# Ten gate tiles of an input projection computed as five pairs of tiles by Strassen's identity

## The chip, the cores and the metric

One core of one Trainium2 chip runs the whole kernel. The metric is device time in microseconds of one execution. All tensors are fp32. A product of two fp32 matrices is done on TensorE as three fp32r products: each operand is first split into a high part (`hi`, a rounded copy that ScalarE writes) and a low part (`lo = x - hi`, which VectorE writes), and then hi·hi, hi·lo and lo·hi are added in PSUM. The profile calls the engines PE (TensorE), PEld (its weight loads), DVE (VectorE), ACT (ScalarE), POOL (GpSimd) and SP (SyncE, which only issues DMAs here).

## The reference, cut to what matters

One decoder layer over L = 1088 columns: 1024 prompt positions and 8 x 8 sample tokens (16 meta tokens stand ahead of them).

```
u = rmsnorm(h, norm_mix)
z = u @ w_in + b_in                       # 48 tiles of 128 columns
a, c, q, k, v, g = split(z)               # g: 24 tiles, three gates of 1024
y_a = pool_mixer(a)                       # moving means, windows 2, 4, 8, 16
y_b = silu(layernorm(conv31(glu(c)))) @ w_conv_out
y_c = attention(q, k, v) @ w_attn_out
gates = sigmoid(g).reshape(.., 3, 1024)
h = h + (gates[0]*y_a + gates[1]*y_b + gates[2]*y_c) @ w_out
h = h + square(relu(rmsnorm(h) @ w_up)) @ w_down
```

A gate tile is thus a product of a 1024x128 block of `w_in` with `u` (1024 x 1088), plus a bias. The kernel stores it in DRAM (`gD`) and reads it back when the gate is used.

## The kernel before

The program order is written by hand: an engine executes its instructions in the order in which the code issues them, and no scheduler changes it. Waits between engines are semaphores; a buffer that is used again waits for its last reader.

**Projection.** `u` lies in SBUF as eight split tiles `Uh[k]`, `Ul[k]` (uh0..uh7, ul0..ul7), 128 rows of the 1024 each. Five tiles are done in a head that also makes `u`; the loop at L1121 does tiles 5 to 47, in the order of the list `TILES`. The last ten, tiles 38 to 47, are gate tiles (kind `z`, z6 to z15). A tile is three chunks of columns (400, 320 and 368 for a gate tile); a chunk is 8 x 3 matmuls with a 128x128 weight block, 72 for the tile. ACT adds the bias and writes `zs` (L916), and the chunk is stored. The weight tile (128x1024) is loaded two tiles ahead, split once (ACT hi at L90, DVE lo at L91), two pairs of buffers.

**What runs beside it.** After each chunk `slot(natt, ndve)` issues one step from the queue `attq` (attention, later the LayerNorm of the convolution) and two from `dveq` (the 31 taps of the depthwise convolution of each of four channel groups, L444 and L446 on DVE, one pair for a tap, and the moving sums of the pooling branch, L463 to L472). The last steps of `attq` are those of the sample attention; then `tail_slices` loads the attention output `oD` and splits it (`Ox`, tiles oh and ol). When the last convolution is through, `after_conv` puts the LayerNorm steps into `attq`.

**After it.** The stage after the projection multiplies the attention output by `w_ao` and the pooled tiles by `w_pool`, multiplies by gates, and adds (AO stage). Then come the conv output, `w_out`, and the MLP.

**Strassen in the MLP.** The up projection already runs in pairs of tiles with seven products in place of eight: `load_pair` loads the two weight tiles of a pair, `sum_pair` makes four sums of 128x512 halves on POOL (L1271 to L1277), `prep` splits one of seven 128x512 operands three products ahead (ACT and DVE, both by the helper `split`, L153 and L154), `product` issues 24 matmuls of 128x272. The operands on the side of the tokens, halves of 544 columns, are split once for all pairs. Evictions (L1590 to L1604) go to ACT and DVE by turns.

Of the kernel before, what the change touches and what calls it, by code (L numbers as in the profile page):

```python
# [7 lines left out]
F32 = mybir.dt.float32  # L8
# [4 lines left out]
P = 128  # L13
# [25 lines left out]
SMP = [0] * 8 + [1] * 6  # L39

# [71 lines left out]
def hybrid_trunk_kernel(ctx, tc, I, O):  # L112
# [56 lines left out]
    W = Weights(nc, pool, page, jobs)  # L169
# [261 lines left out]

    def conv_steps(j):
# [17 lines left out]
    def pool_steps(g):  # L450
# [5 lines left out]
        def add(n, h):  # L456
            def go():
                if n < 2:
                    box[n] = (page("pt"), apool.tile([P, 8, 23], F32, name="pts", tag="pts", bufs=2))
# [16 lines left out]
        dveq.extend([add(n, 1 << n) for n in range(g + 1)] + [fin])  # L476
# [191 lines left out]
    def sample_slices():  # L668
# [3 lines left out]
        def build():  # L672
# [20 lines left out]
            box["os"] = page("os")[:, :512].rearrange("p (j t) -> p j t", j=8)  # L693

        def load(sq):
            r = page("skv")
            kr, vr = r[:, :256].rearrange("p (a s) -> p a s", a=2), r[:, 256:512]
# [18 lines left out]
        def qk(sq):  # L716
# [7 lines left out]
            lg = page("slg")[:, :192]  # L724
# [119 lines left out]
    def proj_open(ti):  # L844
# [5 lines left out]
        elif kind == "c":  # L850
            t["e"] = page("ext")
            t["s"] = apool.tile([P, 8, 38], F32, name="exts", tag="exts", bufs=2)
# [4 lines left out]
        elif kind == "a":  # L857
            t["e"] = page("ea")
            t["s"] = apool.tile([P, 8, 23], F32, name="eas", tag="eas", bufs=2)
# [59 lines left out]
    def proj_close(ti):  # L919
# [31 lines left out]
        elif kind == "q":  # L951
# [65 lines left out]
    def load_split(dst, key, src):  # L1017
        box = {}

        def ld():  # L1020
            box["t"] = page("ld")
# [9 lines left out]
    def tail_slices():  # L1031
        both = lambda *fs: (lambda: [f() for f in fs])
        idle = lambda: None
        pairs = [load_split(Ox, "o", oD[j]) for j in range(8)]
        out = [both(pairs[j][0], pairs[j + 1][0]) for j in (0, 2)]
        for j in range(0, 8, 2):
            fs = [pairs[j][1], pairs[j + 1][1]]
            fs += [pairs[j + 4][0], pairs[j + 5][0]] if j + 4 < 8 else []
            out.append((both(*fs), 1))
        return out  # L1040
# [80 lines left out]
    for ti in range(NHEAD, 48):  # L1121
        if ti == LAST_A + 1:
            dveq.append(after_conv)
        proj_open(ti)
        W.split_to(ti + 2)
        if ti == 47:
            load_gate(2, 0)
            load_gate(0, 0)
        for ci in range(3):
            proj_chunk(ti, ci)  # L1130
            slot(1, NDVE[0] if attq else NDVE[1])
        proj_close(ti)
    while len(Ox) < 8:
        slot(1, 1)
# [79 lines left out]
    apool_ctx.__exit__(None, None, None)  # L1214
    pool2 = ctx.enter_context(tc.tile_pool(name="sb2", bufs=1, reuse_waits="tile"))

    def page2(name):
        return pool2.tile([P, T], F32, name=name, tag="page2", bufs=5)

    HL = L // 2  # L1220
    hD = dram.tile([8, P, L], F32, name="hD")
    BX = ("B11", "T1", "T2", "B22", "T3", "B21", "T4")
# [40 lines left out]

    def sum_pair(j, n):
        a, b = raws[j]
        if n == 0:
            Ssum[j] = page2("s12"), page2("s34")
        s12, s34 = Ssum[j]
        S1, S2, S3, S4 = s12[:, :512], s12[:, 512:1024], s34[:, :512], s34[:, 512:1024]
        if n == 0:  # L1270
            G.tensor_tensor(S1, b[:, :512], b[:, 512:], ALU.add)  # L1271
        elif n == 1:
            G.tensor_tensor(S2, S1, a[:, :512], ALU.subtract)
        elif n == 2:
            G.tensor_tensor(S4, a[:, 512:], S2, ALU.subtract)
        else:
            G.tensor_tensor(S3, a[:, :512], b[:, :512], ALU.subtract)  # L1277

    def prep(s):
        j, i = divmod(s, 7)  # L1280
        a, b = raws[j]
        s12, s34 = Ssum[j]
        src = {"A11": a[:, :512], "A12": a[:, 512:], "A22": b[:, 512:], "S1": s12[:, :512],
               "S2": s12[:, 512:1024], "S3": s34[:, :512], "S4": s34[:, 512:1024]}[ORD[i]]
        tag = ("whi", "wlo")[s % 2]
        t = pool.tile([P, 1024], F32R, name=tag, tag=tag, bufs=2)
        split(t[:, :512], t[:, 512:], src)
        WX[s] = t
        if i == 6:
            raws.pop(j)  # L1290
            Ssum.pop(j)
# [156 lines left out]
    def product(b, s, i, first):  # L1448
        t = WX.pop(s)
        for ch in range(2):  # L1450
            for k in range(4):
# [487 lines left out]
```

## Time and profile before

| | us |
|---|---|
| timed runs: median of three (lowest, highest) | 1669.98 (1669.88, 1670.55) |
| the profiled execution, its own time | 1668.48 |
| its span, first to last instruction | 1666.7 |
| PE busy | 1639.7 (98%) |
| DVE busy | 1109.2 (67%) |
| ACT busy | 748.8 (45%) |
| POOL busy | 413.0 (25%) |

Busy time is summed over the whole span. The shares of DVE, ACT and POOL are means over stages that differ: in one window of the projection DVE is busy all the time, in another a third of it. The profile's chain of waits that ended last is 90% PE.

### The profile page before, as it was taken

How to read it: one execution, taken by the hardware profiler on the slowest of the kernel's cores; microseconds unless marked ns; L12 is line 12 of the kernel's file. 1: busy time of each engine (PE TensorE's matmuls, PEld its weight loads, DVE VectorE, ACT ScalarE, POOL GpSimd, SP SyncE). 2: the span in 40 equal slices, each digit the busy share in tenths (PEclk: the TensorE clock that was granted, in tenths of full speed). 3: DMA queues.
4: the chain of work that ended last, by engine and by line, in shares of the span. 5: the costliest groups of instructions: out<-in, count | busy, mean ns of one | idle time of the engine just before them, and what ended most of it. 6: DMA issues, size and time to landing. Idle time of an engine off the chain costs nothing.

```text
span 1666.7 us, 29169 instructions
## 1 busy us (share of the span) xinstructions
PE 1639.7 (98%) x11552; PEld 1612.8 (97%) x11552; DVE 1109.2 (67%) x1811; ACT 748.8 (45%) x1424; POOL 413.0 (25%) x324
## 2 busy tenths in 40 slices
PE   8999999999999999999999999999999999999997
PEld 7999999999999999999999999999999999999997
DVE  7786767867666575453464698888887844466574
ACT  6537667467665342374243443333333533333331
POOL 1010000001010002122343655555555100023340
PEclk9999999999999999999999999999999999999998
DMA  6051221221225262353243347777776855555642
GB/s 206 16 120 39 83 67 47 68 70 51 70 79 170 93 208 96 107 214 126 80 164 132 131 162 246 246 246 245 243 243 233 323 190 182 183 187 190 232 149 82
DMA packets 132351, 250.80 MB, mean 150 GB/s; under 512 B 33428, under 2 KB 64629, under 8 KB 132213
## 3 DMA queue, kind: packets, MB, share of 16 engines
q1 hardware_dynamic: 132212, 248.92, 45.3%
q8 instruction: 91, 1.49, 0.4%
q14 instruction: 48, 0.39, 0.1%
HBM read 168.52 MB, written 80.36 MB: 149 GB/s over the span
## 4 chain that ended last, share of the span: by engine, by line
PE 90%; DVE 4%; ACT 2%; issue 1%; DMA 1%; POOL 1%; SPq 0%; DVEq 0%; ACTq 0%; POOLq 0%
PE pm L148 12%; PE pm L150 12%; PE pm L149 12%; PE m L1651 6%; PE m L1647 6%; PE m L1649 6%; PE m L1455 6%; PE m L1457 6%; PE m L1458 6%; PE pn L148 3%; PE pn L150 3%; PE pn L149 3%; PE px L622 2%; PE px L610 2%; PE qk L569 2%
## 5 line engine op out<-in xcount | busy, mean ns | idle before, releaser
L148 PE MATMUL pm<-uh,whi 128*128 128x320 f32 (+3 forms) x1008 | 337.7, 335 | 6.6 <-ACT uh L324 6.6
L149 PE MATMUL pm<-ul,whi 128*128 128x320 f32 (+3 forms) x1008 | 331.8, 329 | 0.7 <-DVE ul L325 0.7
L150 PE MATMUL pm<-uh,wlo 128*128 128x320 f32 (+3 forms) x1008 | 331.5, 329 | 0.0
L1647 PE MATMUL m<-oph,whi 128*128 128x272 f32 (+2 forms) x896 | 259.2, 289 | 2.2 <-ACT whi L90 2.2
L1651 PE MATMUL m<-oph,wlo 128*128 128x272 f32 (+2 forms) x896 | 258.8, 289 | 1.8 <-DVE wlo L91 1.8
L1649 PE MATMUL m<-opl,whi 128*128 128x272 f32 (+2 forms) x896 | 258.5, 289 | 0.0
L91 DVE TENSOR_TENSOR wlo<-wraw,whi 128x1024 fp32r<-128x1024 f32 (+1 forms) x127 | 171.1, 1347 | 103.6 <-ACT whi L90 103.5
L90 ACT ACTIVATE whi<-wraw 128x1024 fp32r<-128x1024 f32 (+1 forms) x127 | 130.1, 1025 | 202.3 <-PE m L1649 146.9
L148 PEld LDWEIGHTS pm<-uh,whi 128*128 128x128 f32 x1008 | 190.1, 189 | 8.0 <-ACT uh L324 6.6
L149 PEld LDWEIGHTS pm<-ul,whi 128*128 128x128 f32 x1008 | 190.1, 189 | 3.4 <-DVE ul L325 2.8
L150 PEld LDWEIGHTS pm<-uh,wlo 128*128 128x128 f32 x1008 | 189.9, 188 | 0.2
L1647 PEld LDWEIGHTS m<-oph,whi 128*128 128x128 f32 x896 | 169.3, 189 | 2.6 <-ACT whi L90 2.6
L1651 PEld LDWEIGHTS m<-oph,wlo 128*128 128x128 f32 x896 | 169.2, 189 | 2.6 <-DVE wlo L91 2.5
L1649 PEld LDWEIGHTS m<-opl,whi 128*128 128x128 f32 x896 | 169.4, 189 | 0.0
L444 DVE SCALAR_TENSOR_TENSOR y<-ext,vec,y 128x1024 f32<-128x1024 f32 x120 | 154.5, 1288 | 0.0
L1455 PE MATMUL m<-bch,whi 128*128 128x272 f32 x448 | 129.0, 288 | 3.0 <-DVE cb L1598 2.5
L558 POOL TENSOR_TENSOR uq<-q,uq 128x128 fp32r<-128x128 f32 x64 | 34.7, 564 | 391.9 <-ACT uq L557 391.9
L1455 PE MATMUL m<-bch,wlo 128*128 128x272 f32 x448 | 128.8, 288 | 0.7 <-DVE cb L1598 0.7
L1458 PE MATMUL m<-bch,whi 128*128 128x272 f32 x448 | 128.9, 288 | 0.0
L1458 PE MATMUL m<-bch,wlo 128*128 128x272 f32 x448 | 128.9, 288 | 0.0
L1457 PE MATMUL m<-bcl,wlo 128*128 128x272 f32 x448 | 128.8, 288 | 0.0
L1457 PE MATMUL m<-bcl,whi 128*128 128x272 f32 x448 | 128.8, 287 | 0.0
(365 smaller groups left out, 3804.1 us busy)
## 6 DMA issues: line engine op xcount, KB each, us to landing
wraw<-w_in SPq DMA_DIRECT2D x46, 512.0 KB, 3.8
opT<-d SPq DMA_DIRECT2D x64, 272.0 KB, 3.3
ld<-opT SPq DMA_DIRECT2D x32, 544.0 KB, 4.6
wd<-w_down SPq DMA_DIRECT2D x32, 512.0 KB, 6.4
sumD<-wd SPq DMA_DIRECT2D x32, 512.0 KB, 4.9
wraw<-sumD SPq DMA_DIRECT2D x32, 512.0 KB, 3.6
gt<-gD SPq DMA_DIRECT2D x24, 544.0 KB, 4.6
ld<-opB SPq DMA_DIRECT2D x23, 544.0 KB, 4.8
```

Of the source, the lines that this page charges most:

```text
L90: self.nc.scalar.activation(hi, r, AF.Copy)
L91: self.late.append(lambda lo=lo, r=r, hi=hi: self.nc.vector.tensor_tensor(lo, r, hi.bitcast(F32), ALU.subtract))
L148: PE.matmul(ps, lhsT=wh[k], rhs=xh, start=first and i == 0, stop=False)
L149: PE.matmul(ps, lhsT=wh[k], rhs=xl, start=False, stop=False)
L150: PE.matmul(ps, lhsT=wl[k], rhs=xh, start=False, stop=last and i == n - 1)
L444: V.scalar_tensor_tensor(y[:, :NP], e[:, k:k + NP], w, y[:, :NP], ALU.mult, ALU.add)
L1455: PE.matmul(ps, lhsT=wh, rhs=xh, start=first and k == 0, stop=False, skip_group_check=True)
L1457: PE.matmul(ps, lhsT=wh, rhs=xl, start=False, stop=False, skip_group_check=True)
L1458: PE.matmul(ps, lhsT=wl, rhs=xh, start=False, stop=k == 3, skip_group_check=True)
L1647: PE.matmul(ps, lhsT=wh[:, w], rhs=xh[:, r], start=k == 0, stop=False, skip_group_check=True)
L1649: PE.matmul(ps, lhsT=wh[:, w], rhs=xl[:, r], start=False, stop=False, skip_group_check=True)
L1651: PE.matmul(ps, lhsT=wl[:, w], rhs=xh[:, r], start=False, stop=k == 15, skip_group_check=True)
```

## The change

Tiles 5 to 37 stay as they are. Tiles 38 to 47 become five pairs (numbered -5 to -1) of seven products: 35 products of 24 matmuls of 128x272, 168 matmuls for a pair. Two gate tiles share their token operand, so the identity is on the two tiles, the halves of the 1024 rows (k and k + 4), and the halves of the 1088 columns.

- `z_sums` adds hi and lo of `Uh/Ul[k]` and `[k+4]` back to fp32 (two adds of 128x1088) and makes four differences (128x544) in place. It is called for k = 0 on POOL and k = 1 on DVE when tile 36 opens, for k = 2 on POOL when tile 37 opens, and for k = 3 on DVE after tile 37.
- `z_split` splits these differences (16 splits of 128x544: ACT hi, DVE lo): T1 over the second half of `Uh/Ul[0..3]`, T2 and T3 into `za`, T4 into `zb`.
- Each product evicts two 128x272 pieces: three products on ACT, three on DVE (L1303), the last on ACT with the bias. Two stores a pair, 128x1088 each.
- Weight sums of the first pair are made on DVE, of the others on POOL. Each product has one `prep`, three products ahead.
- Behind each product stands `slot(1, 2)`: one step of `attq` (the splits of T2, T3, T4) and two of `dveq`. When the loop starts, 26 taps of the last convolution are left in `dveq`; the moving sums of the last pooling group are put ahead of them.
- The loads of `oD` and the splits `Ox` move from tiles 38 to 42 into the last pair; the last load (the eighth) is issued behind the store of the last product. `after_conv`, and with it the LayerNorm, moves behind the projection. Tile 37 runs its chunks in the order 1, 2, 0. Some small buffers become parts of pages.

The core of the diff (allocation of small buffers, and functions moved without change, left out):

```
+NZP = 5
+NZ = 48 - 2 * NZP
...
-        dveq.extend([add(n, 1 << n) for n in range(g + 1)] + [fin])
+        fs = [add(n, 1 << n) for n in range(g + 1)] + [fin]
+        if g == 3:
+            dveq[:0] = fs
+        else:
+            dveq.extend(fs)
...
-                attq.append(lambda: wide.append(0))
-                attq.extend(tail_slices())
...
+    def z_sums(k, G):
+        ua, ub = zt[k] = page("zu"), page("zu")
+        lo, hi = slice(0, HL), slice(HL, L)
+        for t, n in ((ua, k), (ub, k + 4)):
+            G.tensor_tensor(t[:, :L], Uh[n][:, NM:].bitcast(F32), Ul[n][:, NM:].bitcast(F32),
+                            ALU.add)
+        G.tensor_tensor(ua[:, lo], ua[:, hi], ua[:, lo], ALU.subtract)
+        G.tensor_tensor(ua[:, hi], ub[:, hi], ua[:, hi], ALU.subtract)
+        G.tensor_tensor(ub[:, hi], ub[:, hi], ua[:, lo], ALU.subtract)
+        G.tensor_tensor(ub[:, lo], ub[:, lo], ub[:, hi], ALU.subtract)
+
+    def z_split(x, k):
...
-    for ti in range(NHEAD, 48):
-        if ti == LAST_A + 1:
-            dveq.append(after_conv)
+    for ti in range(NHEAD, NZ):
         proj_open(ti)
         W.split_to(ti + 2)
-        if ti == 47:
+        if ti == NZ - 2:
+            z_sums(0, G)
+            z_sums(1, V)
+        if ti == NZ - 1:
+            z_sums(2, G)
+        if ti == NZ - 1:
+            load_pair(-NZP)
+        for n, ci in enumerate((0, 1, 2) if ti < NZ - 1 else (1, 2, 0)):
+            if ti == NZ - 1 and n:
+                sum_pair(-NZP, n - 1, V)
+            proj_chunk(ti, ci)
+            if ti == NZ - 1 and n:
+                prep(-7 * NZP + n - 1)
+            slot(1, NDVE[0] if attq else NDVE[1])
+        proj_close(ti)
+    while attq:
+        slot(1, 1)
+    slot(0)
+    z_sums(3, V)
...
+    load_pair(1 - NZP)
+    for k in range(4):
+        z_split("T1", k)
+    prep(-7 * NZP + 2)
+    for n in (2, 3):
+        sum_pair(-NZP, n, V)
+    for x in ("T2", "T3", "T4"):
+        attq.extend(lambda x=x, k=k: [z_split(x, k), z_split(x, k + 1)] for k in (0, 2))
+    oq = [load_split(Ox, "o", oD[j], page2) for j in range(8)]
+    for s in range(-7 * NZP, 0):
+        j, i = divmod(s, 7)
...
+        if s + 3 < 0:
+            prep(s + 3)
+        if j < -1:
+            if 2 <= i < 6:
+                sum_pair(j + 1, i - 2)
+        elif i == 0:
             load_gate(2, 0)
             load_gate(0, 0)
...
+        product(b, s, i, i in (0, 1, 5), z_comb)
...
+            if i < 3:
+                A.activation(d, ps, AF.Copy)
+            elif i == 6:
+                A.activation(d, ps, AF.Identity, bias=bias_col[1])
+            else:
+                V.scalar_tensor_tensor(d, ps, bias_col[i == 4], d, ALU.add, ALU.add)
+        if i > 4:
+            store(gD[TILES[ti + i - 5][1]], c[:, :L])
+        if i == 4 and j < -2:
+            load_pair(j + 2)
+        if j == -1:
...
+            if i > 1:
+                oq[i - 2][1]()
+            for n in (0, 1) if i == 1 else (i,) if i else ():
+                oq[n][0]()
+        slot(1, 2)
+    oq[7][0]()
+    for j in range(5, 8):
+        oq[j][1]()
+    dveq.append(after_conv)
```

Three places of the order follow. A row is line, operation, out<-in with buffer numbers, and the shape; line numbers are each kernel's own. In both kernels y is the convolution's sum (its last group here), `whi`/`wlo` are split weights, `s12` the weight sums S1 and S2.

**DVE, the turn from tile 37 to what follows it.** Before, from the lo of the weights of tile 38 on:

```order
L91 TENSOR_TENSOR wlo_6572<-wraw_6436,whi_6571 128x1024
L444 SCALAR_TENSOR_TENSOR y_4602<-ext_4600,vec_71,y_4602 128x1024
L446 SCALAR_TENSOR_TENSOR y_4602<-exts_4601,vec_71,y_4602 128x64
L444 SCALAR_TENSOR_TENSOR y_4602<-ext_4600,vec_71,y_4602 128x1024
L446 SCALAR_TENSOR_TENSOR y_4602<-exts_4601,vec_71,y_4602 128x64
```

With the change, from the weight sum S2 (ready for the second product) to the first split of T1:

```order
L1076 TENSOR_TENSOR s12_6624<-s12_6624,wraw_6574 128x512
L157 TENSOR_TENSOR whi_6701<-s12_6624,whi_6701 128x512
L453 SCALAR_TENSOR_TENSOR y_4596<-ext_4594,vec_71,y_4596 128x1024
L455 SCALAR_TENSOR_TENSOR y_4596<-xs_4595,vec_71,y_4596 128x64
L453 SCALAR_TENSOR_TENSOR y_4596<-ext_4594,vec_71,y_4596 128x1024
L455 SCALAR_TENSOR_TENSOR y_4596<-xs_4595,vec_71,y_4596 128x64
L1121 TENSOR_TENSOR zu_6710<-uh3_106,ul3_114 128x1088
L1121 TENSOR_TENSOR zu_6711<-uh7_110,ul7_118 128x1088
L1123 TENSOR_TENSOR zu_6710<-zu_6710 128x544
L1124 TENSOR_TENSOR zu_6710<-zu_6711,zu_6710 128x544
L1125 TENSOR_TENSOR zu_6711<-zu_6711,zu_6710 128x544
L1126 TENSOR_TENSOR zu_6711<-zu_6711 128x544
```

Two taps, the six instructions of `z_sums(3)` and then the splits of T1 now stand one behind the other on DVE, ahead of the second product.

**DVE, products 10 to 12 of the 35 (counted from 0).** With the change, from the split for product 13 to the eviction of product 11:

```order
L157 TENSOR_TENSOR whi_7134<-wra_6724,whi_7134 128x512
L1303 SCALAR_TENSOR_TENSOR zc_7027<-zp_7064,b_in_84,zc_7027 128x272
L1303 SCALAR_TENSOR_TENSOR zc_7027<-zp_7065,b_in_84,zc_7027 128x272
L453 SCALAR_TENSOR_TENSOR y_4596<-ext_4594,vec_71,y_4596 128x1024
L455 SCALAR_TENSOR_TENSOR y_4596<-xs_4595,vec_71,y_4596 128x64
L453 SCALAR_TENSOR_TENSOR y_4596<-ext_4594,vec_71,y_4596 128x1024
L455 SCALAR_TENSOR_TENSOR y_4596<-xs_4595,vec_71,y_4596 128x64
L157 TENSOR_TENSOR wlo_7168<-wraw_6936,wlo_7168 128x512
L1303 SCALAR_TENSOR_TENSOR zc_7028<-zp_7029,b_in_84,zc_7028 128x272
L1303 SCALAR_TENSOR_TENSOR zc_7028<-zp_7030,b_in_84,zc_7028 128x272
```

On PE, product 12 ends and product 13 begins so:

```order
L1106 MATMUL zp_7208<-uh7_110,wlo_7099 128x272
L1108 MATMUL zp_7208<-ul7_118,wlo_7099 128x272
L1109 MATMUL zp_7208<-uh7_110,wlo_7099 128x272
L1106 MATMUL zp_7029<-zb_6940,whi_7134 128x272
L1108 MATMUL zp_7029<-zb_6941,whi_7134 128x272
```

Product 13 adds into the bank zp_7029 that the eviction of product 11 has to read first, and that eviction stands on DVE behind all taps and splits issued up to there.

**SP, the end of the pairs.** With the change, the stores of the last two gate tiles and the loads around them:

```order
L224 DMA gD14_143<-zc_7716 128x1088
L1038 DMA ld_7967<-oD_157 128x1088
L224 DMA gD15_144<-zc_7717 128x1088
L1038 DMA ld_7970<-oD_157 128x1088
L1038 DMA ld_7984<-rD0_153 128x1088
L64 DMA wraw_7986<-w_pool 128x1024
```

The eighth load of `oD` (ld_7970) now stands behind the store of gD15, which waits for the last product's eviction; before, all eight were issued in tiles 38 and 39.

## Rows read from the trace of the kernel before

**Rows 1.** The page: busy time, share of the span, instructions of each engine.
```profile
PE 1639.7 (98%) x11552; PEld 1612.8 (97%) x11552; DVE 1109.2 (67%) x1811; ACT 748.8 (45%) x1424; POOL 413.0 (25%) x324
```
**Rows 2.** PE's waits, the longest: what waited for what, us in total, times, longest.
```profile
PE pm L148 <- ACT uh L324: 6.6, 1, 6.6
```
**Rows 3.** Busy time by window: length, engines' us (instructions), PEclk, DMA share, GB/s.
```profile
583.00:594.85 11.85, 11.85 (x74) 11.85 (x73) 4.01 (x5) 2.64 (x5) 0.00 (x0) 1.00 0.70 230
...
618.54:630.39 11.85, 11.85 (x74) 11.85 (x73) 11.85 (x17) 2.65 (x5) 0.00 (x0) 1.00 0.28 91
...
654.08:706.79 52.71, 52.71 (x327) 52.02 (x326) 19.15 (x48) 17.92 (x32) 9.58 (x9) 1.00 0.32 104
583.00:706.79 123.79, 123.79 (x759) 123.10 (x758) 71.33 (x110) 41.79 (x64) 19.11 (x12) 1.00 0.41 138
...
1034.95:1055.97 21.02, 21.02 (x170) 21.02 (x169) 16.97 (x16) 6.48 (x12) 12.37 (x9) 1.00 0.75 241
...
1660.00:1667.00 7.00, 0.00 (x1) 0.00 (x0) 2.44 (x6) 0.38 (x1) 1.41 (x2) 0.50 0.45 152
```
**Rows 4.** Timeline of ACT: start, length, instruction: evictions of gate tiles, of an up pair.
```profile
583.00 0.57 ACT L916 ACTIVATE zs<-pm,b_in 128x368 f32<-128x368 f32 x1 [3.36 <-issue]
...
594.85 0.57 ACT L916 ACTIVATE zs<-pn,b_in 128x368 f32<-128x368 f32 x1 [3.49 <-PE pn L150]
595.31 2.10 ACT L153 ACTIVATE oh<-ld 128x1088 fp32r<-128x1088 f32 x2
...
1034.95 0.63 ACT L1590 ACTIVATE s<-m 128x544 f32<-128x544 f32 x1 [1.87 <-PE m L1458]
```
**Rows 5.** Timeline of PE: a sample attention matmul; first matmuls of two up products.
```profile
559.45 0.50 PE L757 MATMUL spv<-spt,VSh 64*128 64x512 f32 x1
...
1004.71 0.28 PE L1455 MATMUL m<-bch,whi 128*128 128x272 f32 x1
...
1007.72 0.28 PE L1455 MATMUL m<-bch,wlo 128*128 128x272 f32 x1
```
**Rows 6.** Timeline of DVE in the projection: a sample split, two 1088-wide splits, a tap.
```profile
556.67 0.29 DVE L154 TENSOR_TENSOR spt<-str,spt 128x128 fp32r<-128x128 f32 x1 [2.32 <-ACT spt L153]
...
596.45 2.50 DVE L154 TENSOR_TENSOR ol<-ld,oh 128x1088 fp32r<-128x1088 f32 x2 [7.89 <-ACT oh L153]
...
617.25 1.27 DVE L444 SCALAR_TENSOR_TENSOR y<-ext,vec,y 128x1024 f32<-128x1024 f32 x1
618.44 0.27 DVE L446 SCALAR_TENSOR_TENSOR y<-exts,vec,y 128x64 f32<-128x64 f32 x1
618.64 1.27 DVE L444 SCALAR_TENSOR_TENSOR y<-ext,vec,y 128x1024 f32<-128x1024 f32 x1
```
**Rows 7.** Timeline of DVE in an up pair: splits and evictions.
```profile
1039.13 1.76 DVE L154 TENSOR_TENSOR whi<-wraw,whi 128x512 fp32r<-128x512 f32 x1 [1.27 <-ACT whi L153]
...
1045.92 0.71 DVE L1596 TENSOR_TENSOR ca<-m,u 128x544 f32<-128x544 f32 x1
1046.55 0.68 DVE L987 TENSOR_TENSOR wd<-wd 128x512 f32<-128x512 f32 x1
1047.15 0.68 DVE L154 TENSOR_TENSOR whi<-wra,whi 128x512 fp32r<-128x512 f32 x1
1047.75 0.71 DVE L1598 TENSOR_TENSOR cb<-m,s 128x544 f32<-128x544 f32 x1
```
**Rows 8.** Groups of DVE by line and form: count, busy us, mean ns, idle before.
```profile
L1150 DVE SCALAR_TENSOR_TENSOR gt<-pn,vec,gt 128x256 f32<-128x256 f32 x4 | 1.9, 476 | 0.0
```
**Rows 9.** Timeline of POOL: weight sums of an up pair.
```profile
1039.06 1.28 POOL L1271 TENSOR_TENSOR s<-wra 128x512 f32<-128x512 f32 x1
...
1043.70 1.74 POOL L1277 TENSOR_TENSOR s<-wra 128x512 f32<-128x512 f32 x1
```
**Rows 10.** DMA issues: out<-in, count, KB each, median us from issue to landing.
```profile
ld<-oD SPq DMA_DIRECT2D x8, 544.0 KB, 5.0
...
wra<-w_up SPq DMA_DIRECT2D x16, 512.0 KB, 4.2
```

More of the change, by code (lines that the diff above doesn't have):

```diff
@@ L1029, in load_split, with page2 @@
         return ld, sp
[L1031 to L1040, printed above, removed]
+    def page2(name):
+        return pool2.tile([P, T], F32, name=name, tag="page2", bufs=5)
@@ new lines, in prep @@
+    def prep(s):
+        j, i = divmod(s, 7)
+        a, b = raws[j]
+        x = ORD[i]
+        if x[0] == "A":
+            src = {"A11": a[:, :512], "A12": a[:, 512:], "A22": b[:, 512:]}[x]
+        else:
+            n = int(x[1]) - 1
+            src = Ssum[j][n // 2][:, 512 * (n % 2):512 * (n % 2) + 512]
+        tag = ("whi", "wlo")[s % 2]
+        t = pool.tile([P, 1024], F32R, name=tag, tag=tag, bufs=2)
+        split(t[:, :512], t[:, 512:], src)
+        WX[s] = t
+        if i == 6:
+            raws.pop(j)
+            Ssum.pop(j)
@@ new lines, in product @@
+    def product(b, s, i, first, op):
+        t = WX.pop(s)
+        for ch in range(2):
+            for k in range(4):
+                wh, wl = (t[:, o + 128 * k:o + 128 * k + 128] for o in (0, 512))
+                xh, xl = op(BX[i], k, ch)
+                ps = b[ch][:, :HL // 2]
+                PE.matmul(ps, lhsT=wh, rhs=xh, start=first and k == 0, stop=False,
+                          skip_group_check=True)
+                PE.matmul(ps, lhsT=wh, rhs=xl, start=False, stop=False, skip_group_check=True)
+                PE.matmul(ps, lhsT=wl, rhs=xh, start=False, stop=k == 3,
+                          skip_group_check=True)
@@ new lines, in z_split @@
+    def z_split(x, k):
+        lo, hi = slice(0, HL), slice(HL, L)
+        ua, ub = zt[k]
+        if x == "T1":
+            split(Uh[k][:, NM + HL:], Ul[k][:, NM + HL:], ua[:, lo])
+        elif x == "T4":
+            if k % 2 == 0:
+                ZB[k // 2] = page("zb", F32R), page("zb", F32R)
+            c = slice((k % 2) * HL, (k % 2) * HL + HL)
+            split(ZB[k // 2][0][:, c], ZB[k // 2][1][:, c], ub[:, lo])
+        else:
+            if x == "T2":
+                ZA[k] = page("za", F32R), page("za", F32R)
+            c, s = (lo, ub[:, hi]) if x == "T2" else (hi, ua[:, hi])
+            split(ZA[k][0][:, c], ZA[k][1][:, c], s)
@@ new lines, in z_comb, with z_bank @@
+    def z_comb(x, k, ch):
+        o = ch * (HL // 2)
+        if x == "T4":
+            ts, o = ZB[k // 2], o + (k % 2) * HL
+        elif x in ("T2", "T3"):
+            ts, o = ZA[k], o + (x == "T3") * HL
+        else:
+            n = k if x in ("B11", "T1") else k + 4
+            ts, o = (Uh[n], Ul[n]), o + NM + (x in ("T1", "B22")) * HL
+        return tuple(t[:, o:o + HL // 2] for t in ts)
+    def z_bank(*tags):
+        return [psum.tile([P, 512], F32, name="zp", tag=t, bufs=2 if t == "qk" else 3)
+                for t in tags]
@@ new lines, in hybrid_trunk_kernel @@
+    print("left", len(attq), len(dveq))
+    while attq:
+        slot(1, 1)
+    slot(0)
+    z_sums(3, V)
+    apool_ctx.__exit__(None, None, None)
+    pool2 = ctx.enter_context(tc.tile_pool(name="sb2", bufs=1, reuse_waits="tile"))
+    load_pair(1 - NZP)
+    for k in range(4):
+        z_split("T1", k)
[4 more added lines that the diff above has]
+        attq.extend(lambda x=x, k=k: [z_split(x, k), z_split(x, k + 1)] for k in (0, 2))
@@ L1446, in two @@
         return t[:, o:o + HL].rearrange("p (a c) -> p a c", a=2)
[L1448 to L1451, printed above, removed]
-                wh, wl = (t[:, o + 128 * k:o + 128 * k + 128] for o in (0, 512))
-                xh, xl = comb(BX[i], k, ch)
-                ps = b[:, ch, :HL // 2]
-                PE.matmul(ps, lhsT=wh, rhs=xh, start=first and k == 0, stop=False,
-                          skip_group_check=True)
-                PE.matmul(ps, lhsT=wh, rhs=xl, start=False, stop=False, skip_group_check=True)
-                PE.matmul(ps, lhsT=wl, rhs=xh, start=False, stop=k == 3,
-                          skip_group_check=True)
     def square(c):
```

138 lines of the change are left out of this document (75 added, 63 removed).

## The prediction

> **What bounds the kernel now.** I read first the busy shares, then PE's waits, then the stretch that is replaced, window by window. PE is busy 1639.7 of 1666.7 us [rows 1], and its longest wait in the whole trace is 6.6 us, in the head [rows 2]. So TensorE is the bound, and time is gained only where it does less or lost where it is made to stand. The ten tiles that are replaced lie between the last eviction of tile 37 (583.00) and that of tile 47 (706.79): 123.79 us in which PE is busy throughout at a granted clock of 1.00 [rows 3, 4]. The reader is to see a second thing there: in the window of tile 41 DVE is busy 11.85 of 11.85 us with convolution taps, and PE does not wait [rows 3], because an ordinary tile needs one thing of DVE, the lo part of its weights, made two tiles ahead. DVE may run late there for free. Of what follows, the question is whether it still may.
>
> **The change: what is removed from PE.** An ordinary gate tile takes 594.85 - 583.00 = 11.85 us [rows 4]; ten take 118.45 (11.845 by the mean of four such tiles). The window of the ten is 5.3 us longer because the LayerNorm's matmuls fall into the last four (52.71 - 4 x 11.85 = 5.3 [rows 3]); these move behind the projection and cost PE the same there. A pair by Strassen is what the up projection does already, 168 matmuls of the same shape: 21.02 us a pair [rows 3], 1007.72 - 1004.71 = 3.01 us a product [rows 5]. Five pairs: 105.1 us. **PE gains 118.45 - 105.1 = 13.35 us**, if it never stands.
>
> **What DVE must do for it.** Now each product needs DVE every 3.0 us: its weight lo, its token operand's lo, and the eviction of an earlier product from the bank it adds into. All of this stands in one queue with two taps behind each product. I call B the end of tile 37 on PE. The lo split of the second product's weights waits for its hi, which stands on ACT behind the last eviction of tile 37 (0.57 us [rows 4]), the hi's own 0.63 or so (its nearest row is the 128x544 pass, 0.63 [rows 4]) and the passage between engines: DVE stands until about B + 2.0, and all that is queued behind it too. From there to the eviction of product 11, for which product 13 waits, I count in the order:
>
> - 24 taps. One is 618.64 - 617.25 = 1.39 us from start to start [rows 6]: 24 x 1.39 = 33.4 us.
> - `z_sums(3)`: two adds of 1088 columns at 1.25 (half of 2.50, a row of two [rows 6]) and four subtractions of 544 columns at 0.63 (1046.55 - 1045.92 [rows 7]): 5.0.
> - 16 splits of 128x544 (T1 to T4) at 0.63: 10.1.
> - S3 and S4 of the first pair and 13 weight splits, 128x512, at 0.60 (1047.75 - 1047.15 [rows 7]): 1.2 + 7.8.
> - 10 evictions of 128x272 from PSUM. No row has this form; the nearest is 0.476 for 128x256 [rows 8], of which, as with the 0.71 and 0.63 of [rows 7], some 0.08 overlaps with the next: 0.40 each, 4.0.
>
> Sum 61.5 us. DVE does not stand in this stretch (the bank it evicts from was always filled earlier). Product 13 starts at B + 2.0 + 61.5 = B + 63.5 and ends at B + 66.5; without waits it would end at B + 14 x 3.0 = B + 42.0. **PE loses 24.5 us.** PE waits in steps: before product 1 for T1 until about B + 12 (2.0 + 2 taps 2.8 + 5.0 + 4 splits 2.5), then before 2, 4, 6 and at most products up to 13. After that no taps are left, and DVE has 0.6 to 1.4 us a product to do: the last three pairs should run at 21.02 us, as the up pairs do with DVE at 16.97 of 21.02 [rows 3]. A tap that stood later, or one a product, would cost nothing.
>
> **POOL beside it.** A weight split took 1.76 us beside POOL's weight sums against 0.68 alone [rows 7, 9]. Each POOL sum thus sets DVE back by some 1.06 us. In the stretch POOL has the four sums of pair -4 (its weights land about 4.2 us behind their issue [rows 10]) and the four of pair -3: 8 x 1.06 = 8.5 us. Bounds: 0, if they fall where DVE waits, and 12, with two more of pair -2 and 1.2 each; a gain is out, since DVE only waits longer. I take 8.5, since the rows show it for the same instructions.
>
> The Trainium skill ("SBUF — State Buffer", section "Who interferes with whom") says that a DVE instruction with two SBUF inputs and a GpSimd instruction that reads SBUF shut each other out for the whole instruction. By that each sum would cost DVE the sum's own 1.28 us alone, 10.2 us in place of 8.5; the whole would be 1.7 us more. The trace's 1.06 is near it, and no row here tells the two apart.
>
> **The sums before B.** `z_sums(0)` on POOL and `z_sums(1)` on DVE now stand ahead of the last splits of the sample attention. Before, DVE came to that split at 554.35 (it idled 2.32 us to 556.67), and PE used it at 559.45 [rows 5, 6]. With 5.0 us of `z_sums(1)` and some three collisions with POOL (3.2) the split is done at 554.35 + 5.0 + 3.2 + 0.3 = 562.9: **3 us** of PE wait; bounds 0 (the sums slip into idle time) and 8 (all six collide, and PE waits twice).
>
> **The start of the AO stage.** The eighth load of `oD` is issued behind the store of the last product's tile. From the end E of that product: two evictions on ACT and the issues, about 1; landing 5.0 [rows 10]; hi on ACT 1.05 (half of 2.10 [rows 4]); lo on DVE 1.25 (half of 2.50 [rows 6]): ready at E + 8.3. PE does seven of eight row blocks of the first chunk before it needs it: a 416-column chunk is 416/1088 of 11.85, 4.5, so E + 4.0. **4 us** of wait; bounds 0 (an eviction and a landing at their quickest, and other steps in front) and 5.
>
> **Edits at nothing.** Stores of gate tiles, ten weight loads and the reordered chunks of tile 37 stay behind PE's work as before (no row of PE's waits names them); the ACT splits and evictions fit (ACT 6.48 of 21.02 in an up pair [rows 3]). The LayerNorm in the AO stage could add up to 3 us if POOL or its slots come late; I take 0.
>
> **The sum** against the profiled execution: 1668.48 - 13.35 + 24.5 + 8.5 + 3 + 4 = 1695.1. The median of the timed runs lies 1.5 above that execution (1669.98): **1696 us**, 1.6% slower.
>
> **Rivals.**
> *A, the other side: the queue drains in time.* PE's gain of 13.35 stands, and only the 4 us at the AO stage and some of the 3 are lost: 1668.48 - 13.35 + 4 + 1.5 = 1661, at best 1657. It needs the 61.5 us of DVE work, together with POOL's part, to shrink below 24.5 - 13.35 = 11.2 us less, that is to 50: eight taps fewer in the way, or each operation a fifth cheaper. For it speaks that DVE carried the same taps at full load with PE never waiting [rows 3]; against it, that each product now reads what DVE made one or two products before, and that no row has a tap under 1.39. Chance 0.06; a further 0.03 that a milder form ends within 0.2% of before.
> *B, the queue without its neighbours.* POOL's sums fall beside DVE's idle time, and PE is not held before B or at the AO stage: 1681. This and cases between are in the forecast's range.
> *C, the clock.* While PE stood at the end of the kernel its granted clock was 0.50, the 1.2 GHz level [rows 3]. PE stands from about B + 3 to B + 12. If it fell there and products 1 to 13 all ran at that level, 6.0 us each, PE itself would be the bound: B + 12 + 78 = B + 90 in place of B + 75, 15 us more: 1711. Against it: a slow PE is a busy PE, and everywhere else in the trace a busy PE has 1.00. Chance 0.07. The Trainium skill ("TensorE: Matmul & The Clock Gate", section "HAM oscillation — how this bites in real kernels") tells of a kernel whose matmul bursts start at the low clock again after each wait; by that rule C would hold; the windows here show one such fall, at the end, with no matmuls behind it.
>
> **How the numbers follow.** Forecast with its bounds (1681 with the smaller terms at nothing, 1676 if DVE's operations come 8% cheaper too; 1708 with POOL 3.5, the sums before B 5 and the LayerNorm 3 more): 0.84. A and its milder form 0.09, C 0.07. The range 1676 to 1710 takes in the forecast's bounds and leaves out A and most of C. A measurement of this kernel can tell about 0.2% from no change. Faster 0.06, same 0.03, slower 0.91.
>
> **What would show it.** In the profile after: DVE busy at nearly 10 tenths for some 70 us behind tile 37; PE's waits led by lo splits of T1 to T4 and by DVE evictions, all in the first two pairs and together near 33 us; the last three pairs at 21.0 us each; one wait on a split of `oD` at the AO stage; a granted clock below 1.00 in the first pair at most. I am wrong if PE keeps 3.0 us a product in the first two pairs (A), if its waits are as long in the third pair, or if products take 6 us at a low clock (C).

## The result, and the profile after

The changed kernel takes 1713.46 us (median of four runs, 1710.45 to 1715.03) against 1669.93 for the kernel before: ratio 1.0261, 95% interval 1.0248 to 1.0274. It is 43.5 us slower. The forecast was 1696 us, slower by 26, with a range up to 1710: the direction was right, the size was not.

The page of the changed kernel, its busy time and the waits of PE (what waited for what: us in total, times, longest), answer to [rows 1] and [rows 2]:

```profile
PE 1649.0 (96%) x11672; PEld 1617.6 (94%) x11672; DVE 1187.3 (69%) x1898; ACT 770.8 (45%) x1478; POOL 470.7 (27%) x352
```

```profile
PE zp L1108 <- DVE ul L157: 11.5, 1, 11.5
PE zp L1108 <- DVE za L157: 6.6, 3, 3.4
...
PE pm L152 <- DVE ol L157: 5.4, 2, 3.8
PE zp L1106 <- DVE zc L1303: 4.1, 1, 4.1
PE zp L1108 <- DVE zb L157: 3.3, 1, 3.3
...
PE spv L775 <- ACT spt L156: 2.0, 1, 2.0
PE str L763 <- DVE os L758: 1.9, 1, 1.9
```

`zp` is the bank of a product, `ul`, `za` and `zb` are the token operands T1, T2/T3 and T4, `zc` is an eviction, `ol` the attention output, `spv` and `str` are the sample attention. Before, none of these waits was there. To see where the 45.7 us of span went (1712.4 against 1666.7), I cut both traces at three marks: B, the last eviction of tile 37; E, the last eviction of the ten gate tiles; and C, the first DVE instruction of the conv output. ACT's timeline gives B and E:

```profile
591.91 0.59 ACT L934 ACTIVATE zs<-pm,b_in 128x400 f32<-128x400 f32 x1 [3.76 <-issue]
...
692.98 0.49 ACT L1301 ACTIVATE zc<-zp,b_in 128x272 f32<-128x272 f32 x1 [1.02 <-PE zp L1109]
...
714.00 0.49 ACT L1301 ACTIVATE zc<-zp,b_in 128x272 f32<-128x272 f32 x1 [1.02 <-PE zp L1109]
...
735.02 0.49 ACT L1301 ACTIVATE zc<-zp,b_in 128x272 f32<-128x272 f32 x1 [1.02 <-PE zp L1109]
```

| stretch | before | change without waits | after | lost | forecast |
|---|---|---|---|---|---|
| to B | 583.0 | 583.0 | 591.9 | 8.9 | 3 |
| B to E | 118.45 (ten tiles without the LayerNorm) | 105.1 | 143.1 | 38.0 | 33 (24.5 + 8.5) |
| E to C | 110.7 | 116.0 (with the LayerNorm's 5.3) | 125.1 | 9.1 | 4 |
| C to the end | 849.2 | 849.2 | 852.3 | 3.1 | 0 |

59.1 lost less 13.35 won is 45.7. The last two pairs take 21.02 us each (714.00 - 692.98, 735.02 - 714.00), as [rows 3] gave for an up pair: the gain itself is there. From 593.05, where the lo split of the second product's weights starts, to 666.70, the end of product 11's evictions, DVE is busy for 72.05 of 73.65 us and PE for 47.65. In windows of that stretch (length, then busy us of PE, PEld, DVE, ACT, POOL, then PEclk):

```profile
591.90:598.00 6.10, 3.03 (x25) 2.81 (x23) 4.95 (x7) 2.75 (x5) 0.00 (x0) 1.00 0.60 206
598.00:604.00 6.00, 0.00 (x0) 0.00 (x0) 5.90 (x5) 1.18 (x2) 5.65 (x3) 0.64 0.00 0
604.00:610.00 6.00, 3.57 (x16) 3.57 (x17) 6.00 (x8) 0.48 (x1) 1.80 (x2) 0.50 0.00 0
...
622.00:646.00 24.00, 17.28 (x101) 16.62 (x100) 24.00 (x36) 7.45 (x15) 5.66 (x3) 0.79 0.20 71
...
664.00:670.00 6.00, 3.57 (x16) 3.60 (x17) 6.00 (x10) 0.47 (x1) 0.00 (x0) 0.55 0.01 3
...
694.00:715.00 21.00, 21.00 (x170) 21.00 (x169) 7.77 (x13) 7.33 (x15) 0.05 (x1) 1.00 0.13 54
```

Waiting is not all that PE loses. Its granted clock falls to 0.50 in other places too, ahead of B and behind E:

```profile
550.00:560.00 10.00, 8.12 (x39) 7.79 (x38) 8.10 (x18) 3.03 (x10) 6.96 (x5) 0.83 0.10 37
...
570.00:580.00 10.00, 10.00 (x60) 9.75 (x60) 8.62 (x6) 1.61 (x4) 9.89 (x4) 0.88 0.49 178
...
742.00:748.00 6.00, 4.84 (x15) 3.71 (x16) 5.19 (x5) 5.93 (x6) 0.00 (x0) 0.63 1.03 418
```

Before B, PE stands for only 3.9 of the 8.9 us, in the two waits of the sample attention. Behind each of them it is busy throughout at a clock of 0.51, from 555.30 to 558.70 and from 569.00 to 572.50; counting PE's busy time times the missing share of the clock, that is another 3.4 us. The other 1.6 are not accounted for.

### The profile page after: what moved, and what is told of

It reads as the page before. It is cut to its first block, busy times and chain, and to the rows that moved or that the text cites. A ratio compares the mean times of both kernels' runs of the same rounds, so it can differ in the third digit from the quotient of the medians.

```text
span 1712.4 us, 29569 instructions
## 1 busy us (share of the span) xinstructions
PE 1649.0 (96%) x11672; PEld 1617.6 (94%) x11672; DVE 1187.3 (69%) x1898; ACT 770.8 (45%) x1478; POOL 470.7 (27%) x352
## 4 chain that ended last, share of the span: by engine, by line
PE 84%; DVE 8%; issue 3%; ACT 2%; DMA 1%; POOL 1%; SPq 0%; DVEq 0%; ACTq 0%; POOLq 0%
PE pm L151 10%; PE pm L152 10%; PE pm L153 10%; PE m L1781 6%; PE m L1777 6%; PE m L1779 6%; PE m L1108 6%; PE m L1106 6%; PE m L1109 6%; PE pn L151 2%; PE pn L153 2%; PE pn L152 2%; PE px L635 2%; PE px L623 2%; PE qk L582 2%
## 5 line engine op out<-in xcount | busy, mean ns | idle before, releaser
L151 PE MATMUL pm<-uh,whi 128*128 128x320 f32 (+3 forms) x864 | 292.2, 338 | 6.4 <-ACT uh L326 6.4
L152 PE MATMUL pm<-ul,whi 128*128 128x320 f32 (+3 forms) x864 | 287.3, 333 | 0.6 <-DVE ul L327 0.6
L153 PE MATMUL pm<-uh,wlo 128*128 128x320 f32 (+3 forms) x864 | 286.5, 332 | 0.0
L94 DVE TENSOR_TENSOR wlo<-wraw,whi 128x1024 fp32r<-128x1024 f32 (+1 forms) x117 | 163.0, 1393 | 83.4 <-ACT whi L93 83.4
L93 ACT ACTIVATE whi<-wraw 128x1024 fp32r<-128x1024 f32 (+1 forms) x117 | 119.6, 1023 | 176.7 <-PE m L1779 151.3
L151 PEld LDWEIGHTS pm<-uh,whi 128*128 128x128 f32 x864 | 164.6, 191 | 7.5 <-ACT uh L326 6.4
L152 PEld LDWEIGHTS pm<-ul,whi 128*128 128x128 f32 x864 | 164.8, 191 | 3.0 <-DVE ul L327 2.8
L153 PEld LDWEIGHTS pm<-uh,wlo 128*128 128x128 f32 x864 | 164.5, 190 | 0.2
```

The lines of the kernel that those rows point to most:

```text
L93: self.nc.scalar.activation(hi, r, AF.Copy)
L94: self.late.append(lambda lo=lo, r=r, hi=hi: self.nc.vector.tensor_tensor(lo, r, hi.bitcast(F32), ALU.subtract))
L151: PE.matmul(ps, lhsT=wh[k], rhs=xh, start=first and i == 0, stop=False)
L152: PE.matmul(ps, lhsT=wh[k], rhs=xl, start=False, stop=False)
L153: PE.matmul(ps, lhsT=wl[k], rhs=xh, start=False, stop=last and i == n - 1)
```

## The experiments

Times are medians beside runs of the kernel before on the same chip; on the chips used here that kernel's medians lie between 1668.70 and 1669.93 us, so runs are best compared by their ratios. Unless said otherwise a kernel differs from the changed one by its diff alone.

**Are the taps the price of the stretch B to E?**

```
-        slot(1, 2)
+        slot(1, 0 if s + 7 * NZP < 8 else 1)
```

> No tap behind the first eight products, one behind each of the others (26 taps in all, as before). Let B be the last eviction of tile 37 and E that of the last product. Theory (the taps stand in DVE's queue ahead of what the products wait for): the stretch from B to E, 143.1 us in the changed kernel, falls by 17 to 21 us, to 122 to 126 us; what stays is the wait of the second product for T1 (11.5 us) and a few us of a low granted clock. Time 1692 to 1697 us. Rival (the stretch is long because PE runs at the low clock after its first wait, taps or not): it falls by less than 6 us, time above 1707.

Measured: 1700.63 us (ratio 1.0188, 1.0171 to 1.0205), 12.8 less than the changed kernel. B to E is 124.8 us, as the theory said, and the wait for T1 stays at 11.5; the time is 4 us above what I expected, because E to C grew from 125.1 to 130.8: the last taps now run on DVE among the splits of the attention output, and PE waits 5.1 us for a weight split there. The taps are what held the first two pairs; a third of what their delay won was lost again at E.

**Do POOL's weight sums hold DVE up?**

```
+        if -NZP < j < 0:
+            A.activation((S1, S2, S4, S3)[n], (b[:, :512], a[:, :512], a[:, 512:], a[:, :512])[n], AF.Copy)
+            return
```

> The weight sums of the pairs -4 to -1 are left out: ACT copies an operand into their place (a part of the computation is left out). Theory (POOL's sums hold DVE's two-operand instructions up, 8 us in the rows of the stretch): B to E falls by 6 to 9 us, time 1704 to 1708 us. Rival (the collisions fall where DVE or PE waits anyway): under 3 us, time 1710 to 1714.

Measured: 1703.25 us (1.0199, 1.0184 to 1.0214), 10.2 less; B to E 131.9, 11.2 less, a little more than expected. The wait for T1 fell from 11.5 to 7.6. In the changed kernel's timelines of DVE and POOL the collision is plain: the first subtraction of `z_sums(3)` takes 0.72 us and POOL's sum beside it 2.50, where such a sum took 1.28 in [rows 9]; the three behind it take 1.67 each (two are shown):

```profile
598.85 0.72 DVE L1123 TENSOR_TENSOR zu<-zu 128x544 f32<-128x544 f32 x1
599.60 1.67 DVE L1124 TENSOR_TENSOR zu<-zu 128x544 f32<-128x544 f32 x1
```

```profile
598.20 2.50 POOL L1074 TENSOR_TENSOR s<-wra 128x512 f32<-128x512 f32 x1 [15.04 <-DMA wra<-w_in]
600.77 1.62 POOL L1076 TENSOR_TENSOR s<-s,wra 128x512 f32<-128x512 f32 x1
```

**Why is B late?** First the sums were put behind the sample attention in the code, nothing else.

```
-        if ti == NZ - 2:
-            z_sums(0, G)
-            z_sums(1, V)
         if ti == NZ - 1:
+            z_sums(0, G)
             z_sums(2, G)
...
+            if ti == NZ - 1 and n == 1:
+                z_sums(1, V)
```

> z_sums(0) and z_sums(1) are moved from the opening of tile 36 to tile 37, behind the sample attention's chain through DVE; z_sums(2) stays at tile 37. Theory (the 8.9 us by which B comes later than before are these sums on DVE and POOL in the way of the sample attention, two waits of PE, and the low clock behind them): B comes 1 to 2 us late instead of 8.9; time 1705 to 1708 us, if POOL's two sums in a row do not delay T1. Rival (B is late because small buffers were put on pages, or because of the clock alone): B stays 6 us or more late, time above 1710.

Measured: 1714.81 us (1.0273, 1.0258 to 1.0288), no change; B at 592.4. These are the rival's numbers, but for neither of the rival's reasons, as the trace and the next run show. Timelines of POOL and of DVE:

```profile
547.16 6.12 POOL L1121 TENSOR_TENSOR zu<-uh,ul 128x1088 f32<-128x1088 f32 x2 [57.42 <-PE sqk L740]
```

```profile
548.36 2.48 DVE L756 TENSOR_TENSOR ssm<-ssm 128x1 f32<-128x1 f32 x1
550.88 0.16 DVE L757 RECIPROCAL ssm<-ssm 128x1 f32<-128x1 f32 x1
551.08 2.32 DVE L758 TENSOR_SCALAR os<-os,ssm 128x192 f32<-128x192 f32 x1
```

POOL has no other work, so it starts as soon as the page that it writes is free, at 547, although its sums stand behind the sample attention in the code. And one of its 1088-wide adds holds a DVE instruction of one element a partition for 2.48 us; elsewhere in the sample attention the same instruction takes 0.14. So POOL itself has to be held, here by two memsets on one small tile, one on DVE and then one on POOL:

```
+            V.memset(pin, 0.0)
+            G.memset(pin, 0.0)
             z_sums(0, G)
```

> As the run with the sums behind the sample attention, but POOL is also made to wait: a 128x4 memset of DVE behind the pooling steps, then one of POOL on the same tile, stand ahead of z_sums(0). Theory (B is late because POOL, whose queue is empty, starts its 1088-wide sums as soon as their pages are free, wherever the code issues them, and each of them holds a small DVE instruction of the sample attention for up to 2.5 us): B comes at 584 to 586 us instead of 592, time 1705 to 1709 us. Rival (B is late for another reason): B stays above 590.

Measured: 1711.75 us (1.0261, 1.0246 to 1.0276). B came at 583.3, as before the change, and both waits of the sample attention are gone. Against the run just above, from which it differs only by the two memsets, B comes 9.1 us sooner, and the granted clock is 1.00 up to B: POOL's sums had made all of that. In the changed kernel `z_sums(1)` on DVE also stood just ahead of the split for PE's second wait (560.66 to 565.97); its share was not measured apart. The time hardly gained (the ratio is 1.0261 in both), since B to E grew from 143.1 to 149.7. The sums still cost DVE collisions, only later, and what DVE has to make for the products was ready hardly earlier: E is at 733.0 instead of 735.0, and PE now also waits 5.9 us for a weight split. The expected time was wrong there: I had let DVE's work for T1 end at a fixed distance from B, and it does not hang on B.

**Is it the eighth load that makes the AO stage late?**

```
-            for n in (0, 1) if i == 1 else (i,) if i else ():
+            for n in (0, 1) if i == 1 else (5, 6, 7) if i == 5 else (i,) if 0 < i < 6 else ():
...
-    oq[7][0]()
```

> The loads 5, 6 and 7 of the attention output are issued behind product 5 of the last pair, ahead of the last two stores of gate tiles. Theory (the AO stage starts late because the eighth load stands behind the last product's store): the two waits of PE for ol (5.4 us) and the low clock behind them go, 5 to 7 us, time 1706 to 1709 us. Rival (the splits on DVE are late because POOL's LayerNorm sums collide with them there): a wait of 2 us or more stays, gain under 4 us, time 1710 or more.

Measured: 1714.67 us (1.0269, 1.0254 to 1.0285), no change, and the waits for `ol` stand at 5.4 as before: the rival's side. The forecast's reason for its 4 us was wrong in this kernel; what the late load would cost without POOL's sums was not run. DVE and POOL in the changed kernel at that place:

```profile
732.42 2.49 DVE L94 TENSOR_TENSOR wlo<-wraw,whi 128x1024 fp32r<-128x1024 f32 x1
734.83 3.63 DVE L157 TENSOR_TENSOR ol<-ld,oh 128x1088 fp32r<-128x1088 f32 x1
738.38 3.52 DVE L94 TENSOR_TENSOR wlo<-wraw,whi 128x1024 fp32r<-128x1024 f32 x1
```

```profile
731.29 2.53 POOL L499 TENSOR_TENSOR lacc<-y 128x1088 f32<-128x1088 f32 x1 [37.25 <-PE zp L1109]
733.91 6.91 POOL L501 TENSOR_TENSOR lacc<-lacc,y 128x1088 f32<-128x1088 f32 x2
```

The LayerNorm moved behind the projection brings its three sums on POOL to just this place; three DVE instructions that take 1.2 to 1.3 us each alone took 9.6 together. Held behind the last split by the same two memsets, on top of the early loads:

> As the run with the early loads of the attention output, and the LayerNorm's first sums on POOL (lacc) are held by two memsets until the last split of the attention output on DVE is done. Theory (those three 1088-wide sums, 9.4 us of POOL, hold the splits up, not the loads): PE's two waits for ol at the start of the AO stage (5.4 us) fall under 1.5 us; time 1705 to 1709 us, if the LayerNorm is not late for it. Rival (ACT or the loads set the splits): the waits stay above 3 us.

Measured: 1707.81 us (1.0238, 1.0220 to 1.0255), 6.9 less than with the early loads alone (some 5 by the ratios). E to C falls from 125.1 to 120.9, the waits for `ol` from 5.4 to 1.7, near the bound I gave. Another 3.0 lie behind C (848.8 against 851.8), which the last section comes to.

**Is it the clock?** PE stands 11.5 us before the second product, and its granted clock falls to 0.50 there. Dummy matmuls fill the gap:

```
+        if s == -7 * NZP:
+            fill = z_bank("px")[0]
+            for n in range(80):
+                PE.matmul(fill[:, :HL // 2], lhsT=wt[:, :128], rhs=Uh[0][:, NM:NM + HL // 2],
+                          start=True, stop=True, skip_group_check=True)
```

> 80 matmuls of 128x272 that nobody reads, some 10 us, are put on PE behind the first product, where it waits 11.5 us for T1; all else as in the changed kernel. Theory (the clock falls while PE waits, but DVE's queue sets the pace of the first two pairs): the granted clock between B + 3 and B + 25 rises to 1.00, and B to E falls by 0 to 3 us, to 140 to 143 us; time 1710 to 1714 us. Rival (the low clock behind that wait is what makes the stretch long): B to E falls by 6 us or more, time below 1708.

Measured: 1713.06 us (1.0268, 1.0252 to 1.0283), no change. In the windows of this kernel the clock is 1.00 through the gap and the first product behind it (604 to 610, 0.50 without the filler); it fell later, in the next gaps, so the expected rise to B + 25 was only partly there:

```profile
598.00:604.00 6.00, 5.81 (x46) 5.58 (x45) 5.90 (x5) 1.18 (x2) 5.84 (x4) 1.00 0.01 3
604.00:610.00 6.00, 3.92 (x23) 3.06 (x23) 5.62 (x8) 1.64 (x4) 0.64 (x1) 1.00 0.00 0
610.00:622.00 12.00, 8.35 (x44) 7.51 (x45) 10.64 (x16) 5.98 (x14) 0.00 (x0) 0.72 0.11 28
```

B to E is 143.4. In this gap the low clock cost nothing, since DVE set the pace. The run does not speak for the later falls, nor for those ahead of B and behind E.

**A better order.** The next kernel joins the above: POOL's `z_sums` held, `z_sums(3)` and half of T1 ahead of tile 37's last chunk, weight sums on DVE, no taps behind products 0 to 4 and mostly one behind 5 to 28, early loads, lacc held.

```
-        slot(1, 2)
+        p = s + 7 * NZP
+        slot(1, 0 if p < 5 or p > 28 else 2 if p in (7, 13, 14, 20, 21, 27) else 1)
...
-                sum_pair(j + 1, i - 2)
+                sum_pair(j + 1, i - 2, V)
```

> All together: POOL's sums held behind the sample attention and the pooling steps; z_sums(3) and two splits of T1 ahead of the last chunk of tile 37; the weight sums of the pairs on DVE; no taps behind products 0 to 4, one behind most of 5 to 28, two behind six of them; early loads of the attention output; lacc held. Theory: B at 584 to 587, B to E 108 to 116 us, the AO stage late by under 4 us; time 1660 to 1672 us. Rival (DVE has too much to do in the five pairs for any order): B to E above 122 us, time above 1680.

Measured: 1680.05 us (1.0066, 1.0051 to 1.0081): B at 583.1, but B to E 123.0, on the rival's side, and PE still waits 10.0 us for T1. The rival's reason, too much work for any order, does not hold, as the next run shows. DVE's timeline shows what POOL's held sums do now to `z_sums(1)`, a weight split and a tap between 571 and 585:

```profile
571.26 1.76 DVE L1124 TENSOR_TENSOR zu<-zu 128x544 f32<-128x544 f32 x1
...
578.48 2.83 DVE L157 TENSOR_TENSOR wlo<-wraw,wlo 128x512 fp32r<-128x512 f32 x1
581.23 3.58 DVE L453 SCALAR_TENSOR_TENSOR y<-ext,vec,y 128x1024 f32<-128x1024 f32 x1
```

So POOL was taken out of `z_sums` altogether (all four on DVE at tile 37, with all four splits of T1 ahead of its last chunk; its two taps move behind later products):

```
+            if ti == NZ - 1 and n == 0:
+                z_sums(0, V)
+                z_sums(1, V)
             if ti == NZ - 1 and n == 1:
+                z_sums(2, V)
```

> As the spread version, but z_sums(0) and z_sums(2) are on DVE too, behind the sample attention, so that POOL does nothing there, and the two taps that stood in tile 37 move behind later products. Theory (in the spread version POOL's held sums still cost DVE some 17 us between 561 and 595 us, more than the 10 us that DVE needs to make them itself): PE's wait for T1 falls from 10.0 to under 4 us, B to E from 123.0 to 109 to 114 us; time 1664 to 1672 us. Rival (DVE has no less to do, the wait only moves): B to E above 118 us, time above 1676.

Measured: 1672.09 us (1.0018, 1.0009 to 1.0027), 8.0 less though DVE does more work; B to E 113.4, and the wait for T1 is gone from the list. The move of T1's splits and of the two taps is part of the 8.0. The first of those instructions, without POOL beside it:

```profile
565.56 0.72 DVE L1124 TENSOR_TENSOR zu<-zu 128x544 f32<-128x544 f32 x1
```

Then the loads and splits of the attention output were started before the last pair:

```
+            oq[i][1]()
+            for n in (i + 2,) if i < 5 else (7,) if i == 5 else ():
+                oq[n][0]()
...
+        if j == -2 and i in (4, 5):
+            oq[i - 4][0]()
```

> As the version with all sums on DVE; the loads of the attention output begin two products before the last pair (the first two into other pages) and one split stands behind each product of the last pair, so that one is left at its end. Theory (the AO stage starts late since three splits are left at E): the stretch from E to the conv output falls by 2 to 4 us against the version without this; time 1662 to 1670 us. Rival (the transfers are the limit there, or the splits hold the last pair up): no gain, or B to E longer by as much.

Measured: 1670.29 us (1.0005, 0.9996 to 1.0014), not to be told from the kernel before; E to C fell from 120.8 to 118.5, as the theory said. The price of POOL's weight sums against DVE's own, in this order:

```
-                sum_pair(j + 1, i - 2, V)
+                sum_pair(j + 1, i - 2)
```

> As the version before, but the weight sums of the pairs -4 to -1 are on POOL again. Theory (a POOL sum of 512 columns costs a DVE instruction some 1.06 us, DVE's own sum 0.60): slower by 16 x 0.46, up to 7 us where DVE is the bound, 2 to 7 us in all. Rival (POOL takes work off DVE): faster by 3 us or more.

Measured: 1676.06 us (1.0043, 1.0029 to 1.0057): 5.8 slower, B to E 120.4 against 113.5. DVE loses more by POOL's sums than it spends on making them.

Last, in the first pair the product that needs no token sum was put second, with its weights split ahead of T1:

```
+    ORD1 = ("A11", "A12", "S1", "S2", "S4", "S3", "A22")
```

> As the version whose loads of the attention output begin before the last pair (which took as long as the kernel before), but in the first pair the product A12 x B21, which needs no sum of tokens, runs second, and its weights are split ahead of T1. Theory (what is left is PE's gap at the second product, 4 us with the low clock behind it, and 2 us of waits at T2 and T3): B to E falls from 113.5 to 107 to 110 us; time 1664 to 1668 us, 0.1 to 0.3% faster than before. Rival (the gap moves to the third product): B to E above 112 us, time 1669 to 1672.

Measured: 1666.44 us, ratio 0.9981 (0.9972 to 0.9990): 0.2% faster than the kernel before, the only version here that beats it. B to E is 110.7, just above what I expected. Its first four windows of 21 us behind tile 37 show what is left to win:

```profile
583.00:604.00 21.00, 19.21 (x146) 18.15 (x144) 20.90 (x36) 13.34 (x28) 0.00 (x0) 1.00 0.38 122
604.00:625.00 21.00, 19.41 (x152) 19.18 (x153) 21.00 (x34) 7.05 (x15) 0.00 (x0) 1.00 0.28 92
625.00:646.00 21.00, 21.00 (x170) 21.00 (x169) 21.00 (x34) 7.34 (x15) 0.00 (x0) 1.00 0.29 97
646.00:667.00 21.00, 21.00 (x169) 20.94 (x168) 21.00 (x36) 7.32 (x15) 0.00 (x0) 1.00 0.33 115
```

PE loses 3.4 us in the first two windows, and DVE is busy for 83.9 of 84.0 us: in these four windows it has no room left.

## Why the prediction was right or wrong

- **The gain on PE, 13.35 us: right.** Undisturbed pairs take 21.02 us, in the place of 23.7.
- **DVE's queue in the first two pairs, 24.5 us, and POOL beside it, 8.5: right in kind and nearly in size.** From the lo split of the second product's weights (593.05, which is B + 1.1 and not B + 2.0) to the end of product 11's evictions (665.80 + 0.90 = 666.7) 73.6 us passed; my sum was 61.5 + 8.5 = 70. DVE stood for 1.6 us of them, which I had put at nothing, and ten of POOL's sums fell into the stretch, not eight. The run with the taps put later and the run without POOL's weight sums show the two shares (18.3 and 11.2 us of B to E). E came 5.0 us later than the sum said: those 3.6, less the earlier start, and product 13, which took 5.5 us in place of 3.0 at a granted clock of 0.55 (666.43 to 671.90).
- **The sums before B, 3 us: the term that was mis-sized, 8.9.** I priced three collisions by 1.06 us (the rows give 1.76 - 0.68 = 1.08), a price from 512-wide instructions on both engines. Beside a POOL add of 1088 columns a DVE instruction took up to 2.5 us, however small it was (2.48 in place of 0.14), and the sample attention's chain is made of small ones. I also took the code's place for POOL's sums as their time; POOL's queue is empty there and runs ahead. PE stood for 3.9 us, near the 3 forecast, but partly by luck: the first wait (1.9) is one that the term did not look for. Another 3.4 went at the low clock behind the two waits, for which the term had nothing. With `z_sums(1)` moved behind and POOL held, waits and low clock were gone and B came at 583.3.
- **The start of the AO stage, 4 us: the size too small (9.1) and the reason wrong.** Moving the eighth load alone changed nothing; holding the LayerNorm's sums on POOL as well took 4.2 us away. I had looked at these sums only as something that PE would wait for ("if POOL or its slots come late"), not as something that stops DVE. From E to C PE stood for 6.9 us, 5.4 of them for `ol`, and worked at a clock of 0.54 from 739.20 to 746.70, up to 1.7 us more. With POOL held PE still stood for 3.8 us there; that rest was not taken apart.
- **The step that failed.** The profiled span is 19 us longer than the sum gives: 5.9 before B, 5.0 from B to E, 5.1 at the AO stage, 3.1 behind C. Two things were wrong in the terms. First, POOL beside DVE was costed for one pair of forms and one place; where it was not, holding POOL took 9.1 us off ahead of B and 4.2 behind E. Second, the terms count only the time for which PE stands, as if it came back at full clock. Some 11 of the 19 us are PE's own work at the low clock: 3.4 before B, 2.5 in product 13, up to 1.7 at the AO stage, 3.4 in the first up pair. The ground given against a slow clock, that "everywhere else in the trace a busy PE has 1.00", was a misreading: in the trace of the kernel before PE is busy for 3.40 of 3.40 us at 0.51 from 1609.80 to 1613.20, right behind waits of 1.8 and 0.7 us. The sign "a granted clock below 1.00 in the first pair at most" failed with it. The falls ahead of B and at the AO stage were gone in the runs with POOL held; why the clock fell in the up pair stays open.
- **On the skill's rule** the prediction said that no row told it from 1.06 us a collision. In the run with the sums behind the sample attention, 0.14 us became 2.48 beside a 1088-wide add, which takes 2.53 us on POOL where nothing holds it up: a whole instruction of POOL, and not a fixed price. What the Trainium skill ("SBUF — State Buffer", section "Who interferes with whom") says, that a DVE instruction with two SBUF inputs and a GpSimd instruction that reads SBUF shut each other out for the whole instruction, agrees with these rows.
- **Rival C (the clock): not the cause of the stretch B to E.** Its time, 1711, was near the measured one by luck. The filler kept the clock up behind the first gap and gained nothing, and B to E went with DVE's work. But the clock had a share in the miss, as said above, mostly outside the stretch for which C was written.
- **Rival A (the queue drains in time): no.** It came about only with a queue made for it, in the last kernels.

## What to carry to other kernels

When a change makes the bound engine depend every few microseconds on another, add up that engine's queue in order up to each thing waited for, not its total: here DVE was busy for 106.6 of the 143.1 us of the five pairs, and yet PE was 38 us late after fourteen products. Work "beside" DVE on POOL is not free where DVE reads two SBUF operands: taking sixteen 512-wide sums back from POOL gained 5.8 us, and taking back two sets of `z_sums`, with a better place for T1's splits and two taps, gained 8.0. A wait can also cost more than its length: where PE is the bound, look at the granted clock behind it. And an instruction on an idle engine's queue runs when its inputs and its buffer are ready, not where the code puts it; to place it in time it needs something to wait for.

## What was not expected of the hardware

- A DVE instruction with one tensor operand and a column of scalars was held too: the 128x192 one at 551.08, in the run with the sums behind the sample attention, took 2.32 us, where it takes 0.32 in the undisturbed chain.
- Behind C the changed kernel lost 3.1 us. In the first up pair its granted clock was 0.91 in a window, and 1.00 in the window of before that answers to it, with the same busy time of PE and 25 fewer matmuls done in it:

```profile
1020.00:1060.00 40.00, 37.52 (x279) 37.33 (x278) 33.70 (x45) 10.18 (x18) 16.41 (x11) 0.91 0.60 200
```

```profile
976.00:1016.00 40.00, 37.47 (x304) 37.29 (x303) 36.50 (x46) 11.34 (x20) 18.99 (x12) 1.00 0.63 219
```

  From C to the end the kernels took 848.8 to 852.8 us with the same code. Every profiled execution has such falls there (the last 14 us, where PE mostly stands, not counted), some 1.7 us lost in each, and the time goes with their number: 848.8 to 850.8 us in the six kernels with one, 850.9 to 852.7 in the six with two, 852.3 and 852.8 in the two with more. The kernel before has one as well, near its end. Why the same short waits (2.5 us at the longest in the first up pair, in both kernels) let the clock fall in one kernel and not in another was not settled here.
